# Four edits at the start of a mixture-of-experts stage: tile memory, an earlier second gather group, the scale folded into the stored tokens, block sums dealt out

## The chip, the core and the metric

The kernel runs on 1 core of one Trainium2 chip, as one program. A run's time is the device time of that core, in microseconds (us). Times are told as the median of several runs; the profile is of one further execution.

## The reference, cut to what matters

Two layers work on 512 tokens of width 1024. Each mixes the tokens (layer 0: attention beside pooling; layer 1: spatial gating beside a short convolution), projects the result out, adds it to the stream, and then runs a mixture of 16 experts, of which every token uses two of one group.

```python
h_lat = h_lat + g1 * y                                # y: the mixer with its out-projection
h_lat = h_lat + g2 * hier_moe(modulate(h_lat, norm2_g[i], sh2, sc2), *moe_args)

def modulate(x, gain, shift, scale):
    return rms_norm(x, gain) * (1 + scale) + shift

def hier_moe(t, ...):
    g_idx = top_k(softmax(t @ rg_w + rg_b), 1)        # the group
    top_i = top_k(softmax(e_logits of that group), 2) # two experts in it
    # per expert: y = (silu(t @ wg) * (t @ wu)) @ wd, added with the token's weight
```

## The kernel before, in words

The engines are called by their short names: PE multiplies matrices, DVE and ACT work on vectors, POOL issues gathers and scatters, SP issues the loads of weights. Each engine does its instructions in the order in which they are written.

**Out-projection (out_proj, L1081).** For each of four tiles of 128 tokens (t = 0 to 3) and each half of the width, PE makes 128x512 products; DVE multiplies them by the gate row (L1124, tile yo) and adds them to the stream h (L1125); ACT squares h for the norm (L1127, junk); PE turns h round and forms the router's logits. When a tile has its norm, store (L1151) scales h by it on ACT into a tile u, of which there are three, and sends u to device memory (td, 512 KB a tile), from POOL's queue for t = 0 to 2 and from ACT's for t = 3.

**Routing (route, L1228).** From the logits lg DVE ranks groups and experts (bt, rk, ohg), marks the two chosen (Ab, L1254), PE sums these marks into places (hp), and DVE makes pa (each token's place with each expert) and cnt (tokens of each expert). That is the first part of route; its second part (L1268 to L1300) works out the weights of the tokens and writes them into rec. All tiles of routing lie in the pool "mt", whose memory was in part that of u and of the rest of the out-projection.

**Experts (experts, L1372).** Each expert is a unit with up to 128 tokens, in two halves of 64 (k = 0, 1); the second half runs only if the expert has over 64 tokens. onehot (L1344) makes 128x512 masks oh on DVE; slots (L1352) multiplies them with rec on PE, which gives the tokens' numbers, and DVE decodes them (idxf, idxs, idx); rows (L1582) lets POOL gather 64 double rows of td into a tile gath. unit_t (L1589) then has PE transpose a gathered tile (tp), and ACT and DVE each apply scale and shift to half of it (tf, lines L1601 and L1603: four operations of 128x64 on each, because each column block has a scale and a shift of its own in m2). gu_half (L1610) multiplies tf with the gate and up weights (gu), gated makes hm from it, hidden turns it round (hp, then hf), and down (L1635) multiplies by the down weights (yp), from where DVE weighs the result (ys) and POOL adds it to the stream in device memory.

**The order around the change.** PE, ACT and DVE run in written order in this stage. first_group (L1404) decodes units 0 and 1 one tile at a time, reads the counts into registers (counts, L1465), runs the second part of route, loads ACT's table of silu, and transposes units 0 and 1. Then come unit 0's gate and up products, then second_group (L1427), which makes masks for units 2 and 3 and gathers their tokens, and then the loop over units p. PLAN (L165) is a table of the extra work that follows the gate and up products of unit p + 1: ("o", a) makes masks for units a and a + 1, ("t", a) decodes them, ("w", a) decodes weights, ("r", i) is a third of route_extra (L1302), which counts the further blocks of 128 tokens that crowded experts need. In layer 0 two further blocks are straight units (STRAIGHT = (2, 0)), and the "r" entries are worked off at p = 3, 4 and 5. Layer 1 has none, and there all of route_extra runs at once after p = 5 (end of the loop). Loads of weights go round 16 buffers (raw_any, L258): raw tiles, one raw tile of a pool that reuses u's memory (raw3), halves of h, and the tiles wh and wl.

## Time and profile before

| what | us |
|---|---|
| median of 3 runs (lowest, highest) | 927.77 (925.64, 930.54) |
| the profiled execution | 927.96 |
| its span | 925.8 |
| PE busy in the span | 827.0 (89%) |
| DVE, ACT, POOL busy | 499.4, 335.9, 224.5 |
| mean granted clock of PE | 0.946 of full speed |

The span runs from the first to the last instruction that the profile holds; the 2.2 us around it belong to the execution's time. In the rows below each time is in us from the span's start. In a timeline's row the brackets tell how long the engine was idle just before, and which engine or transfer ended that. SPq, POOLq and ACTq are transfers issued from these engines' queues.

### The profile page before, as it was taken

To read this page: it belongs to the slowest core of one execution; us is meant where nothing else is said; L and a number is where in the kernel's file an instruction comes from. 1 tells how busy PE (TensorE), PEld (TensorE's weight loads), DVE (VectorE), ACT (ScalarE), POOL (GpSimd) and SP (SyncE) were. 2 spreads that over 40 slices of the span, in tenths; PEclk is the share of its full clock that TensorE was granted. 3 is DMA by queue.
4 is the path that set the end of the run, shared out by engine and by line. 5 is a ranking of instruction groups with operands and counts; after the bars stand their busy time and mean duration, and the time that the engine had idled before them with its cause. 6 is when DMAs were issued, how large, how long until landed. Compare 5 with 4: busy or idle time off the path is not lost. (4 is left out here: it accounts for less than half of the span.)

```text
span 925.8 us, 14465 instructions
## 1 busy us (share of the span) xinstructions
PE 827.0 (89%) x5352; PEld 538.3 (58%) x5352; DVE 499.4 (54%) x1236; ACT 335.9 (36%) x710; POOL 224.5 (24%) x196
## 2 busy tenths in 40 slices
PE   6999889999997679999977699999997679899993
PEld 2786557766885345455543487777786335445451
DVE  5467757677344645663322787776444554543330
ACT  4356456557235522223221442223235522222320
POOL 1002220021000234776234000000000255734332
PEclk9999999999999689999999799999999679999997
DMA  9755345454918667999998556882827568999731
GB/s 376 287 195 224 148 166 183 149 182 163 370 59 286 199 210 234 332 319 309 329 318 295 187 205 196 282 306 103 310 111 276 196 233 280 350 318 342 266 44 26
DMA packets 50706, 216.70 MB, mean 234 GB/s; under 512 B 12996, under 2 KB 13508, under 8 KB 32816
## 3 DMA queue, kind: packets, MB, share of 16 engines
q1 hardware_dynamic: 31392, 187.09, 55.0%
q0 software_dynamic: 16736, 21.36, 10.3%
q10 hardware_dynamic: 2480, 6.95, 2.0%
q8 instruction: 60, 0.98, 0.4%
q14 instruction: 38, 0.31, 0.1%
HBM read 207.95 MB, written 26.25 MB: 253 GB/s over the span
## 5 line engine op out<-in xcount | busy, mean ns | idle before, releaser
L1614 PE MATMUL gu<-raw,tf 128*64 128x256 f32 x1072 | 139.4, 400 | 7.5 <-DMA raw<-wgu 4.7
L1614 PEld LDWEIGHTS gu<-raw,tf 128*64 128x64 f32 x1072 | 76.5, 143 | 59.7 <-issue 22.5
L1601 ACT ACTIVATE tf<-tp,m 128x64 f32<-128x64 f32 x192 | 67.0, 401 | 85.2 <-DVE tf L1603 43.7
L1603 DVE TENSOR_SCALAR tf<-tp,m 128x64 f32<-128x64 f32 x192 | 57.1, 339 | 73.6 <-ACT tf L1601 72.6
L290 ACT CAST wh<-raw 128x1024 fp32r<-128x1024 f32 x46 | 48.1, 1049 | 94.8 <-PE acc L609 52.3
L291 DVE TENSOR_TENSOR wl<-raw,wh 128x1024 fp32r<-128x1024 f32 x46 | 55.8, 1219 | 40.1 <-ACT wh L290 40.1
L1641 PE MATMUL yp<-raw,hf 128*64 128x512 f32 x272 | 72.1, 653 | 1.0 <-ACTq L1561 0.4
L1622 ACT ACTIVATE sg<-gu 128x128 f32<-128x128 f32 x48 | 13.3, 277 | 155.2 <-PE gu L1614 120.5
L608 PE MATMUL acc<-xh,wh 128*128 128x512 f32 x160 | 64.2, 402 | 0.3 <-DVE vn L1022 0.3
L610 PE MATMUL acc<-xh,wl 128*128 128x512 f32 x160 | 63.8, 399 | 0.5 <-DVE wl L291 0.5
L609 PE MATMUL acc<-xl,wh 128*128 128x512 f32 x160 | 63.9, 399 | 0.0
L1584 POOL DMA_INDIRECT gath<-td,idx x48 | 52.3, 1089 | 19.5 <-issue 11.0
L1644 DVE SCALAR_TENSOR_TENSOR ys<-yp,w,bc_g 128x512 f32<-128x512 f32 x34 | 25.4, 747 | 52.7 <-PE yp L1641 38.1
L1651 POOL DMA_INDIRECT out<-ys,idx x24 | 37.5, 1564 | 63.1 <-DVE hm L1624 53.1
L1348 DVE TENSOR_TENSOR oh<-cst,pa 128x512 bf16<-128x512 f32 x80 | 50.1, 683 | 0.0
L1651 POOL DMA_INDIRECT hd<-ys,idx x24 | 39.0, 1623 | 34.8 <-DVE hm L1624 14.9
L515 DVE SCALAR_TENSOR_TENSOR acc<-raw,silu_c,acc 128x1024 f32<-128x1024 f32 x28 | 35.8, 1280 | 17.9 <-ACT acc L513 9.2
L1595 PE MATMUL tp<-cst,gath 128*128 128x128 f32 x192 | 34.7, 310 | 11.6 <-DMA gath<-td,idxs 7.5
L537 POOL DMA_DIRECT2D rowd<-row x4 | 2.4, 596 | 173.6 <-DVE row L531 90.5
L1595 PEld LDWEIGHTS tp<-cst,gath 128*128 128x128 f32 x192 | 22.6, 153 | 33.4 <-issue 22.9
L1624 DVE TENSOR_TENSOR hm<-gu,sg 128x128 f32<-128x128 f32 x48 | 13.8, 288 | 47.9 <-ACT sg L1622 47.5
L300 DVE TENSOR_TENSOR pl<-tp,ph 128x384 fp32r<-128x384 f32 x64 | 34.0, 551 | 8.3 <-ACT ph L299 8.0
(318 smaller groups left out, 1748.4 us busy)
## 6 DMA issues: line engine op xcount, KB each, us to landing
raw<-modw SPq DMA_DIRECT2D x48, 1024.0 KB, 6.2
raw<-wgu SPq DMA_DIRECT2D x48, 1024.0 KB, 7.5
raw<-wdn SPq DMA_DIRECT2D x24, 1024.0 KB, 7.1
raw<-wodd SPq DMA_DIRECT2D x10, 1024.0 KB, 6.7
h<-wgu SPq DMA_DIRECT2D x8, 1024.0 KB, 6.6
wh<-wgu SPq DMA_DIRECT2D x12, 512.0 KB, 8.6
wl<-wgu SPq DMA_DIRECT2D x12, 512.0 KB, 7.5
raw<-woe SPq DMA_DIRECT2D x4, 1024.0 KB, 4.8
```

Of the source, the lines that this page charges most:

```text
L291: last_lo = nc.vector.tensor_tensor(lo, src, hi.bitcast(F32), op=ALU.subtract).ins
L608: t.matmul(out, ah, bh, start=start, stop=False, skip_group_check=True)
L609: t.matmul(out, ah, bl, start=False, stop=False, skip_group_check=True)
L610: t.matmul(out, al, bh, start=False, stop=stop, skip_group_check=True)
L1348: self.nc.vector.tensor_tensor(oh, io[:, None, None, :].to_broadcast([128, NT, 2, 64]), pos[:, :, None, None].to_broadcast([128, NT, 2, 64 ...
L1584: self.gather[u] = self.nc.gpsimd.indirect_dma_start(out=self.gbuf[u % len(self.gbuf)][:, k], out_offset=None, in_=self.td, in_offset=bass ...
L1595: nc.tensor.transpose(tp[:, c], g[:, k, c * 128:(c + 1) * 128], self.ident)
L1601: nc.scalar.activation(tf[:, c, cs], tp[:, c, cs], AF.Identity, bias=m[:, 1, j, c:c + 1], scale=m[:, 0, j, c:c + 1])
L1603: nc.vector.tensor_scalar(tf[:, c, cs], tp[:, c, cs], m[:, 0, j, c:c + 1], m[:, 1, j, c:c + 1], op0=ALU.mult, op1=ALU.add)
L1614: self.nc.tensor.matmul(gu[64 * j:64 * j + 64], tf[:, k4, 64 * c:64 * c + 64], ws[c][k4 // 2][:, k4 % 2 * 512 + j * 256:k4 % 2 * 512 + j * ...
L1641: nc.tensor.matmul(yp[64 * c:64 * c + 64], hf[:, 64 * j:64 * j + 64], ws[2][j][:, c * 512:c * 512 + 512], start=(j == 0), stop=(j == 1), t ...
L1651: s = self.nc.gpsimd.indirect_dma_start(out=self.acc, out_offset=bass.IndirectOffsetOnAxis(ap=idx, axis=0), in_=self.ys[p % len(self.ys)][ ...
```

## The change

1. **Tiles.** Routing's first tiles (rec, rk, ohg, Ab, pa, cnt) go into R0, the pool that was current before the experts' pool was opened; E1, E2 and the rest stay in the experts' pool.
2. **Second group.** second_group is called in first_group right behind counts, ahead of unit_t for units 0 and 1 and of the second part of route and the table load. unit_t of unit 2 and the last zeros move to PLAN[0] between "w" and the second "o". zeros reads a constant instead of h.
3. **Scale.** The row of the scale is broadcast to all partitions (bc_s2, a further transfer on POOL), update multiplies h by it into u (scaled, a 128x512 operation on DVE), u has four buffers, store scales u in place. unit_t is then one DVE operation of 128x512 that adds the shift.
4. **Block sums.** Layer 1 works off route_extra by the "r" entries at p = 3, 4 and 5, as layer 0 does.

```diff
-PLAN = {0: (("o", 0), ("w", 0), ("o", 4)), 1: ...
+PLAN = {0: (("o", 0), ("w", 0), ("u", 2), ("o", 4)), 1: ...
...
     def bcasts(self, eng=None):
-        self.bcast("g1", self.bcp, eng)
+        for nm in ("g1", "s2"):
+            self.bcast(nm, self.bcp, eng)
...
+            def scaled(t, half):
+                cs = slice(half * 512, (half + 1) * 512)
+                if not half:
+                    us[t] = S.tile([128, D], F32, name="u", bufs=4)
+                return nc.vector.tensor_tensor(us[t][:, cs], self.h[:, t, cs], self.bc["s2"][:, cs], op=ALU.mult).ins
...
-                last = nc.vector.tensor_tensor(self.h[:, t, cs], self.h[:, t, cs], z, op=ALU.add).ins
+                nc.vector.tensor_tensor(self.h[:, t, cs], self.h[:, t, cs], z, op=ALU.add)
+                last = scaled(t, half)
...
             def store(t, r, q=None):
-                u = S.tile([128, D], F32, name="u", bufs=3)
-                nc.scalar.activation(u, self.h[:, t], AF.Copy, scale=r)
-                (q or nc.gpsimd).dma_start(tdv[t], u)
+                nc.scalar.activation(us[t], us[t], AF.Copy, scale=r)
+                (q or nc.gpsimd).dma_start(tdv[t], us[t])
...
     def moe(self, l):
+            self.R0 = self.R
             R = self.R = self.pool(es, f"mt{l}")
...
     def route(self, R, pp):
+        M, R = R, self.R0
         rec = R.tile([128, NE, NT, 5], BF16, name="rec")
...
-        Ab, E1, E2 = T4("Ab", BF16), T4("E1"), T4("E2")
+        Ab = T4("Ab", BF16)
...
         yield pa, rec, cnt
+        R = M
+        E1, E2 = T4("E1"), T4("E2")
...
             self.regs = counts()
+            second_group()
             zeros(self.gbuf[4:6])
+            for u in range(2):
+                th[u, 0] = self.unit_t(u, 0, S, pp)
             next(rt)
             self.table(AF.Silu)
-            for u in range(2):
-                th[u, 0] = self.unit_t(u, 0, S, pp)
-            zeros(self.gbuf[6:] + [y[:, 1:2] for y in self.ys])
...
-            second_group()
             regs = self.regs
...
+                    if what == "u":
+                        th[2, 0] = self.unit_t(2, 0, S, pp)
+                        zeros(self.gbuf[6:] + [y[:, 1:2] for y in self.ys])
...
                     elif what == "r":
-                        if nst:
-                            rx = rx or self.route_extra(R, tb)
-                            next(rx)
+                        rx = rx or self.route_extra(R, tb)
+                        next(rx)
...
-                if not p:
-                    th[2, 0] = self.unit_t(2, 0, S, pp)
...
-                if p == 5 and not nst:
-                    rx = list(self.route_extra(R, tb))
...
     def unit_t(self, u, k, S, pp):
-        m = self.m2[self.l]
-        for j in range(2):
-            cs = slice(64 * j, 64 * j + 64)
-            for c in range(2):
-                nc.scalar.activation(tf[:, c, cs], tp[:, c, cs], AF.Identity, bias=m[:, 1, j, c:c + 1], scale=m[:, 0, j, c:c + 1])
-            for c in range(2, 4):
-                nc.vector.tensor_scalar(tf[:, c, cs], tp[:, c, cs], m[:, 0, j, c:c + 1], m[:, 1, j, c:c + 1],
-                                        op0=ALU.mult, op1=ALU.add)
+        sh = self.m2[self.l][:, :, :, None].to_broadcast([128, 4, 2, 64])
+        nc.vector.tensor_tensor(tf.rearrange("p c (j s) -> p c j s", j=2), tp.rearrange("p c (j s) -> p c j s", j=2), sh,
+                                op=ALU.add)
```

In the lists of instructions that follow, "..." leaves rows out. First DVE where layer 0's experts begin, before (cnti are the counts, TENSOR_LOAD their reading into registers, E to rec the second part of routing):

```order
L1468 CAST cnti<-cnt 1x16
L1471 TENSOR_LOAD cnti x4
L1270 SCALAR_TENSOR_TENSOR E_3144<-rk,ohg 128x64
L1271 SCALAR_TENSOR_TENSOR E_3145<-rk,ohg 128x64
...
L1299 CAST rec<-wq 128x64
L1603 TENSOR_SCALAR tf<-tp,m_0_103 128x64 x8
L1348 TENSOR_TENSOR oh<-cst,pa 128x512 x4
L1365 TENSOR_REDUCE idxs<-hp 128x4
L1624 TENSOR_TENSOR hm<-gu,sg 128x128
L1348 TENSOR_TENSOR oh<-cst,pa 128x512 x4
```

The same place now, with the lines' new numbers:

```order
L1480 CAST cnti<-cnt 1x16
L1483 TENSOR_LOAD cnti x4
L1360 TENSOR_TENSOR oh<-cst,pa 128x512 x4
L1377 TENSOR_REDUCE idxs<-hp 128x4
L1607 TENSOR_TENSOR tf<-tp,m_0_103 128x512 x2
L1282 SCALAR_TENSOR_TENSOR E_3341<-rk,ohg 128x64
...
L1311 CAST rec<-wq 128x64
L1628 TENSOR_TENSOR hm<-gu,sg 128x128
L1360 TENSOR_TENSOR oh<-cst,pa 128x512 x4
L1381 TENSOR_REDUCE wf_3454<-hp 128x4
L1607 TENSOR_TENSOR tf<-tp,m_0_103 128x512
L1360 TENSOR_TENSOR oh<-cst,pa 128x512 x4
```

The masks and the decoding of the second group (oh, idxs) stand right behind the counts, and the two shift additions (tf) ahead of the second part of routing. hm of unit 0 stands behind that part, as unit 0's gate and up products no longer have the second group behind them; unit 2's tf stands ahead of the masks of the second "o". Layer 1 begins with the same rows.

Second, DVE in layer 1 around the block sums (nb to cx), before:

```order
L1644 SCALAR_TENSOR_TENSOR ys_8241<-yp,w_8745,bc_g_7775 128x512
...
L1307 TENSOR_SCALAR nb<-cnt 128x16
...
L1313 COPY cs<-nb 128x16
L1317 TENSOR_TENSOR cs<-cs 128x16 x4
...
L1330 TENSOR_REDUCE xe<-selt 128x7
L1334 CAST nx<-cs 1x1
...
L1340 TENSOR_REDUCE cx<-selt 1x7
L1624 TENSOR_TENSOR hm<-gu,sg 128x128
L1603 TENSOR_SCALAR tf<-tp,m_1_104 128x64 x4
```

And now:

```order
L1319 TENSOR_SCALAR nb<-cnt 128x16
...
L1325 COPY cs<-nb 128x16
L1360 TENSOR_TENSOR oh<-cst,pa 128x512 x4
...
L1381 TENSOR_REDUCE w_8891<-hp 128x4
L1329 TENSOR_TENSOR cs<-cs 128x16 x4
...
L1342 TENSOR_REDUCE xe<-selt 128x7
L1572 COMPARE_AND_BRANCH
L1607 TENSOR_TENSOR tf<-tp,m_1_104 128x512
...
L1360 TENSOR_TENSOR oh<-cst,pa 128x512 x4
L1346 CAST nx<-cs 1x1
...
L1352 TENSOR_REDUCE cx<-selt 1x7
L1572 COMPARE_AND_BRANCH
```

The 19 operations that stood in one row, between two units, are three pieces behind the decoding or the masks of three units.

Third, SP's loads while layer 0's out-projection ends (h is the stream's tile, used as a buffer for weights; wh and wl too), before:

```order
L255 DMA raw<-wdn 128x2048
L274 DMA wh<-wgu 128x1024
L255 DMA raw<-wgu 128x2048
L274 DMA wh<-wdn 128x1024
L274 DMA wh<-wgu 128x1024
L255 DMA raw<-wgu 128x2048
L269 DMA h<-wgu 128x2048
L274 DMA wl<-wgu 128x1024
...
L269 DMA h<-wdn 128x2048
```

And now:

```order
L255 DMA raw<-wdn 128x2048
L269 DMA h<-wdn 128x2048
L274 DMA wh<-wgu 128x1024
L255 DMA raw<-wgu 128x2048
L274 DMA wh<-wdn 128x1024
L274 DMA wh<-wgu 128x1024
L255 DMA raw<-wgu 128x2048
L269 DMA h<-wgu 128x2048
L274 DMA wl<-wgu 128x1024
```

The 1 MB load `h<-wdn` has moved from behind the wl loads to the front: zeros no longer reads h, so nothing behind the out-projection holds it. Beside these, the fixed order of attention's and pooling's products in layer 0 comes out otherwise on PE, ACT and DVE, with the same products.

## Rows read from the trace of the kernel before

**Rows 1.** The profile page, section 2: the span in 40 equal slices of 23.1 us. Each digit is a tenth: PE's busy share, and the clock that PE was granted.

```profile
PE   6999889999997679999977699999997679899993
...
PEclk9999999999999689999999799999999679999997
```

**Rows 2.** Busy time by stretch. A row gives the stretch and its length, then busy us (and instructions) of PE, of PE's weight loads, of DVE, ACT and POOL, then PE's granted clock, the DMA engines' busy share and GB/s.

```profile
120.00:246.00 126.00, 121.32 (x855) 87.90 (x854) 87.78 (x223) 73.70 (x165) 11.99 (x13) 0.99 0.53 195
...
356.00:470.00 114.00, 111.42 (x867) 58.96 (x863) 57.02 (x169) 31.04 (x101) 66.92 (x50) 1.00 0.99 321
...
766.00:807.30 41.30, 41.23 (x340) 21.77 (x334) 20.34 (x55) 10.81 (x35) 26.79 (x21) 1.00 0.96 325
```

**Rows 3.** Timeline of layer 0 from the last tile's store to the first gate and up products (start, duration, engine, line, operation, count, idle before).

```profile
298.23 0.33 ACTq L1154 DMA_DIRECT2D td<-u  x1
...
301.70 0.33 SPq L255 DMA_DIRECT2D raw<-wgu  x1
303.01 0.23 DVE L1254 SCALAR_TENSOR_TENSOR Ab<-rk,ohg 128x64 bf16<-128x64 f32 x1 [4.09 <-DMA td<-u]
...
305.32 0.15 DVE L1365 TENSOR_REDUCE idxf<-hp 128x1 int32<-128x2 f32 x1
...
306.32 1.58 POOL L1584 DMA_INDIRECT gath<-td,idxf  x1 [2.80 <-DVE idxf L1365]
...
310.41 0.23 DVE L1270 SCALAR_TENSOR_TENSOR E<-rk,ohg 128x64 f32<-128x64 f32 x1 [2.00 <-issue]
...
311.84 1.09 PE L1595 MATMUL tp<-cst,gath 128*128 128x128 f32 x4 [0.26 <-DMA gath<-td,idxf]
...
314.22 5.25 PE L1614 MATMUL gu<-raw,tf 128*64 128x256 f32 x32 [1.29 <-ACT tf L1601]
...
314.85 0.26 DVE L1299 CAST rec<-wq 128x64 bf16<-128x64 f32 x1
```

**Rows 4.** The same timeline, from the second group's masks on.

```profile
318.79 2.49 DVE L1348 TENSOR_TENSOR oh<-cst,pa 128x512 bf16<-128x512 f32 x4
...
321.63 0.17 DVE L1365 TENSOR_REDUCE idxs<-hp 128x4 int32<-128x8 f32 x1 [0.35 <-PE hp L1358]
321.71 0.33 SPq L269 DMA_DIRECT2D h<-wdn  x1
321.89 0.29 DVE L1624 TENSOR_TENSOR hm<-gu,sg 128x128 f32<-128x128 f32 x1
...
322.54 0.33 PE L1630 MATMUL hp<-cst,hm 128*128 128x128 f32 x1
```

**Rows 5.** The timeline of layer 0 from the last weight slots to the transposes of unit 2 and of unit 0's second half.

```profile
324.64 0.25 PE L1358 MATMUL hp<-rec,oh 128*128 128x3 bf16 x4 [0.35 <-DVE oh L1348]
...
328.58 1.97 PE L1595 MATMUL tp<-cst,gath 128*128 128x128 f32 x8 [3.69 <-DMA gath<-td,idxs]
```

**Rows 6.** Timeline of layer 1's first stretch.

```profile
720.75 0.23 DVE L1254 SCALAR_TENSOR_TENSOR Ab<-rk,ohg 128x64 bf16<-128x64 f32 x1 [4.42 <-DMA td<-u]
...
724.01 1.60 POOL L1584 DMA_INDIRECT gath<-td,idxf  x1 [3.11 <-DVE oh L1348]
...
727.88 0.23 DVE L1270 SCALAR_TENSOR_TENSOR E<-rk,ohg 128x64 f32<-128x64 f32 x1 [1.76 <-issue]
...
739.39 0.29 DVE L1624 TENSOR_TENSOR hm<-gu,sg 128x128 f32<-128x128 f32 x1
```

**Rows 7.** Timeline of layer 1, last weight slots and transposes.

```profile
742.15 0.25 PE L1358 MATMUL hp<-rec,oh 128*128 128x3 bf16 x4 [0.35 <-DVE oh L1348]
...
746.18 1.12 PE L1595 MATMUL tp<-cst,gath 128*128 128x128 f32 x4 [3.78 <-DMA gath<-td,idxs]
```

**Rows 8.** Timeline of layer 1 at the block sums, behind unit 5: their first operation, and PE's next two.

```profile
806.46 0.17 DVE L1307 TENSOR_SCALAR nb<-cnt 128x16 f32<-128x16 f32 x1
...
811.66 0.33 PE L1630 MATMUL hp<-cst,hm 128*128 128x128 f32 x1 [4.32 <-DVE hm L1624]
...
811.92 1.57 PE L1614 MATMUL gu<-raw,tf 128*64 128x256 f32 x8
```

**Rows 9.** PE's timeline in layer 0 at the units where the block sums are dealt out there.

```profile
375.15 1.08 PE L1614 MATMUL gu<-wh,tf 128*64 128x256 f32 x8 [0.67 <-DVE ys L1644]
...
388.67 1.08 PE L1614 MATMUL gu<-wl,tf 128*64 128x256 f32 x8 [0.78 <-DVE tf L1603]
```

**Rows 10.** The profile page, section 5: the two groups of operations in unit_t (busy us, mean ns of one, idle time before them and what ended most of it).

```profile
L1601 ACT ACTIVATE tf<-tp,m 128x64 f32<-128x64 f32 x192 | 67.0, 401 | 85.2 <-DVE tf L1603 43.7
L1603 DVE TENSOR_SCALAR tf<-tp,m 128x64 f32<-128x64 f32 x192 | 57.1, 339 | 73.6 <-ACT tf L1601 72.6
```

**Rows 11.** DVE's groups by line and form in 258 to 296 us, layer 0's out-projection.

```profile
L1124 DVE TENSOR_TENSOR yo<-sp,bc_g 128x512 f32<-128x512 f32 x8 | 5.2, 686 | 12.3 <-PE sp L610 12.2
```

**Rows 12.** DVE's waits in the same stretch (us in total, times, longest).

```profile
DVE ss L1137 <- ACT junk L1127: 0.9, 1, 0.9
```

**Rows 13.** Transfers issued in 296 to 332 us: what, from which queue, how many, median us from issue to landing.

```profile
gath<-td,idxf POOLq DMA_INDIRECT x4, 3.7
```

**Rows 14.** PE's waits in 356 to 497 us, the loaded part of layer 0's experts (us in total, times, longest).

```profile
PE gu L1614 <- DMA raw<-wgu: 4.7, 1, 4.7
```

**Rows 15.** PE's waits in 120 to 246 us, layer 0's attention and pooling.

```profile
PE sp L878 <- ACT pe L887: 1.2, 1, 1.2
```

**Rows 16.** ACT's groups by line and form in 140 to 246 us: the exponentials of attention.

```profile
L887 ACT ACTIVATE pe<-sp,nb 128x768 f32<-128x768 f32 x27 | 24.5, 907 | 5.5 <-DVE nb L883 3.9 <-DVE ed L966 1.1 <-DVE ri L915 0.2
```

More of the change, by code (lines that the diff above doesn't have):

```diff
@@ L164 @@
 WE, WR, WS = (32, 20), (0, 0, 4), (12, 24)
-PLAN = {0: (("o", 0), ("w", 0), ("o", 4)), 1: (("t", 4), ("o", 2), ("w", 2), ("o", 6)), 2: (("t", 6), ("o", 8)),
+PLAN = {0: (("o", 0), ("w", 0), ("u", 2), ("o", 4)), 1: (("t", 4), ("o", 2), ("w", 2), ("o", 6)), 2: (("t", 6), ("o", 8)),
         3: (("t", 8), ("r", 0), ("o", 10)), 4: (("t", 10), ("r", 1)), 5: (("o", 12), ("r", 2)), 6: (("t", 12), ("x", 0)),
@@ L369, in setup @@
         self.gather = {}
-        self.m2 = [k.tile([128, 2, 2, 4], F32, name=f"m2_{l}") for l in range(2)]
+        self.m2 = [k.tile([128, 4, 2], F32, name=f"m2_{l}") for l in range(2)]
         self.ends = None
@@ L469, in router_parts @@
         if j0 == 0:
-            nc.vector.tensor_copy(self.m2[l][:, 0], cp)
             nc.vector.tensor_tensor(rw, rw, cp[:, :, :, None].to_broadcast([128, 2, 4, 20]), op=ALU.mult)
             return
-        col = self.m2[l][:, 1]
+        col = self.m2[l].rearrange("p f j -> p j f")
         nc.vector.tensor_copy(col, cp)
@@ L540, in bcasts @@
     def bcasts(self, eng=None):
-        self.bcast("g1", self.bcp, eng)
+        for nm in ("g1", "s2"):
+            self.bcast(nm, self.bcp, eng)
     def bcast(self, nm, pool, eng=None):
         t = pool.tile([128, D], F32, name="bc_" + nm)
-        src = self.rowd[self.l, 0:1, 0:2].rearrange("a j n -> a (j n)")
+        G, j = {"g1": (0, 0), "s2": (1, 0)}[nm]
+        src = self.rowd[self.l, G:G + 1, j:j + 2].rearrange("a j n -> a (j n)")
         (eng or self.nc.gpsimd).dma_start(t, src.to_broadcast([128, D]))
@@ L1101, in out_proj @@
             pl = pp.tile([128, 512], F32, name="po")[:, :80].rearrange("p (t n) -> p t n", n=20)
+            us = {}
             ssq = self.sm.tile([128, 2, NT], F32, name="ssq", bufs=1)
@@ L1443, in zeros @@
                 t = t.rearrange("p b d -> p (b d)")
-                nc.scalar.activation(t, self.h[:, 0, :t.shape[-1]], AF.Copy, scale=0.0)
+                nc.scalar.activation(t, self.ident[:, 0:1].to_broadcast([128, t.shape[-1]]), AF.Copy, scale=0.0)
         def weights(a):
@@ L1516, in experts @@
                 for what, a in PLAN.get(p, ()):
-                    if what == "w":
+                    if what == "u":
+                        th[2, 0] = self.unit_t(2, 0, S, pp)
+                        zeros(self.gbuf[6:] + [y[:, 1:2] for y in self.ys])
+                    elif what == "w":
                         weights(a)
```

## The prediction

> **What bounds the kernel now.** I began with the page's slices. PE is busy at 9 tenths in most of them, with a low in slices 13 and 14 (278 to 324 us) and in 32 and 33 (717 to 764 us), and there its granted clock falls as well [rows 1]. These are the two places where the experts of a layer begin. Next, the stretches: in the middle of the experts PE works in 111.42 of 114.00 us and in 41.23 of 41.30 us, in attention in 121.32 of 126.00 us [rows 2]. An operation taken from DVE or ACT in those stretches is worth nothing; the two starts are where time can be had. So I read their timelines. The reader is to see three stops in each. DVE has ohg done and sits 4.09 us before Ab, until a store of u has landed [rows 3]; in layer 1 it is 4.42 us [rows 6]. Then the second group's masks come on DVE only when units 0 and 1 are under way [rows 4]. And PE stands 3.69 and 3.78 us before the transposes of unit 2, until its gather has landed [rows 5, 7]. A fourth stop is in layer 1 alone: PE waits 4.32 us for hm, while DVE works off the block sums [rows 8].
>
> **Layer 0's start.** I shift the rows along DVE, because all that PE does here hangs on it.
>
> 1. Ab no longer waits: 303.01 - 4.09 = 298.92 us. From Ab to the first idxf are 2.31 us [rows 3], so the first list is there at 301.2. The gather can't follow at once, since it reads td: the last store is issued at 298.23, and Ab's own wait ended with its landing at 303.0. So the 4.09 us of the wait become 303.0 against 306.32, a gain of 3.3 us for the gather, and 4.09 us for what hangs on DVE alone.
> 2. After the counts DVE is free at 310.41 - 4.09 = 306.3 [rows 3]. The masks of the second group now stand there: from their start to idxs 2.84 us [rows 4], so slots and idxs are done by 309.2. They are on the path now, but were on it before as well.
> 3. The gathers of units 0 and 1 start at 303.0 and 1.9 us later (1.58 and a gap of 0.3 on POOL) and land 3.7 us on [rows 3, 13]: 306.7 and 308.6. PE comes to the transposes at 309.1, so they are hidden, with 0.5 to 2 us to spare. Two transposes at 1.09 [rows 3] end at 311.3.
> 4. The additions: 128x512 from PSUM. The nearest row is yo, of that shape and source, at 0.686 us [rows 11]; the eight operations that it replaces took 401 and 339 ns each in turn between ACT and DVE [rows 10]. First products at about 311.1 against 314.22, second addition done at 312.1.
> 5. The second part of routing, from E to the end of rec, took 310.41 to 315.11 = 4.70 us [rows 3]. It now lies behind the additions: 312.1 to 316.8. hm of unit 0 stands behind it, and so starts at 316.8, not at 321.89 [rows 4]: 5.1 us earlier. PE idles some 2 us before it; that is in the sum.
> 6. From hm to the transposes of unit 2 the work is the same up to the last slots (324.64 [rows 5]); the wait of 3.69 us behind them goes, since idxs now is there at 309.2 and its gathers land by 315. Gain at unit 2: 5.1 + 3.69 = **8.8 us**.
>
> **Layer 1's start.** By the same steps: E would be at 727.88 - 4.42 = 723.46 [rows 6]; the masks there instead, idxs 2.84 later at 726.3; first gather at 720.75, when the store has landed, against 724.01; the second's landing at 720.75 + 1.9 + 3.7 = 726.4, no later than PE's turn. Two transposes at the full clock, some 0.65 each, and the addition: 728.3. Routing's second part 4.7: hm at 733.0 against 739.39 [rows 6], 6.4 us; with the wait of 3.78 [rows 7] **10.2 us**.
>
> **Block sums.** The 4.32 us stop goes. Behind it PE took 1.57 us for eight products [rows 8] that take 1.08 us elsewhere [rows 9], since its clock had fallen; with the transposes and down products behind, I estimate the aftermath at 1.3 (0.49 here, and about 0.4 for each of two further groups of such a size). Dealt out, the sums cost what layer 0's show: stops of 0.67 and 0.78 us [rows 9]. 5.6 - 1.45 = **4.2 us**. Bounds: 2.5, if the clock gives nothing back (4.32 - 1.45 = 2.9) and a third piece shows, and 5.6.
>
> **What it costs.** scaled adds a 128x512 operation of about 0.69 us per half tile (by yo [rows 11], as the nearest). Behind it stands the sum of squares ss, which waited for ACT's squaring by 0.9 us [rows 12]; one scaled fits in, for t = 0 and 1 two stand there, so 0.4 us a layer, **0.8 us** in all; bounds 0 and 16 x 0.69 = 11 us, the former nearer, as most of these lie under PE's products (DVE sat 12.2 us before yo [rows 11]). The broadcast of bc_s2 on POOL is wanted only behind attention's 126 us [rows 2] and is priced at nothing; without that cover it would be one more wait of a transfer, some 4 us by [rows 13]. `h<-wdn` moves from 321.71 [rows 4] to the out-projection on SP; it takes its 1 MB out of the start of the experts and puts it beside the out-projection, priced at nothing, with 1 us either way. In the loaded middle the lighter unit_t is priced at nothing, with at most the 2.6 us that PE idles in 114 [rows 2] as a bound. Layer 0's attention comes in another order: its products are the same, and I put 0, bounds -3 and +3 from PE's 4.7 us of idle time there [rows 2].
>
> **The sum.** -8.8 - 10.2 - 4.2 + 0.8 = -22.4 us. The profiled execution took 927.96 us, 0.2 over the median, so 905.6 there and **905.4** for a median.
>
> **Rivals.**
>
> A. Layer 0 gives it back to the stream of weights. For: in 356 to 470 us the DMA engines are busy 0.99 of the time [rows 2], and PE has a stop of 4.7 us for a load behind it [rows 14]; if the stream doesn't start earlier too, that stop grows by all of layer 0's gain. Against: the loads are released when PE gives buffers back, and so shift with it. 905.4 + 8.8 = 914.2. Chance 0.13.
>
> B. The first gathers collide with a load. The load of raw3 was issued at 301.70, when two stores of u had landed, 4.6 us ahead of the first gather [rows 3]; now it and the gather wait for the same last store, and 1 MB goes out beside them. Gathers that take as long again, 3.7 us [rows 13], eat the spare time of 0.5 to 2 us and put off the transposes by some 2.5 us a layer: 910.4. The Trainium skill, "DMA: Bandwidth & Descriptors", section "Queues, rings and completion order", says that each DMA engine takes turns between the queues that have work for it, packet by packet; by that rule the gathers would get about half of the engines for as long as the load is under way, which is the doubling of this case and would make the sum -17.4 in place of -22.4. The rows here don't decide it, as no load went out with the first gathers before. Chance 0.12.
>
> C. The change doesn't free the tiles: R0's memory is held by something else of the out-projection, or the masks oh wait for u's memory in their turn. Then the starts win only the second group's part (the 3.69 and 3.78 us, and its slots) and lose 4.09 and 4.42: 905.4 + 8.5 = 913.9. Chance 0.04.
>
> D. Slower: the new order of layer 0's attention. PE does its rows in order; there it stood 1.2 us for an exponential on ACT, once [rows 15], of 27 at 0.907 us each [rows 16]. If the new order puts products ahead of an exponential that isn't done, each costs about that 1.2 us; all 27 would make 32 us, 937.8. It decides from 23 of the 27 on (22.4 us of gain and 4.6 of margin). Against: PE has work from three other chains there, and idles 4.7 of 126 us. Chance 0.04. With half of them and A, the time would lie at 920 to 928, about no change: 0.05.
>
> **How the numbers follow.** My forecast, 0.62. Down, the aftermath of the block sums and the clock (1.4), the attention (3), and the lighter units (2 to 3) reach to 897; up, A, B and C reach to 915, and A with B to 918. Range 897 to 918. The measurement can tell about 0.5%, 4.6 us: faster below 923.1, slower above 932.4. Forecast, A, B and C lie below 923: 0.91; D above: 0.04; the mixture between: 0.05.
>
> **What would show it.** In the changed profile: Ab right behind ohg in both layers, with no wait on td<-u; first gathers when the last store has landed, some 3.3 us earlier; idxs ahead of the first gu; no wait of PE before unit 2's transposes; a stop of some 2 us of PE before unit 0's hm, behind routing's second part; in layer 1 no stop of over 1 us at the block sums; ACT's share of unit_t gone, with PE's busy time in the middle unchanged. The forecast is wrong if Ab or oh waits as long as before, if the gathers take over 6 us, if the stop for a load in layer 0 [rows 14] grows by the start's gain, or if PE's idle time in layer 0's attention grows by over 5 us.

## The result, and the profile after

| what | us |
|---|---|
| changed kernel, median of 4 runs (lowest, highest) | 895.78 (891.66, 899.29) |
| kernel before, beside it, 4 runs | 926.70 (922.86, 930.54) |
| ratio, 95% interval | 0.967 (0.961 to 0.972) |
| the profiled execution of the changed kernel, its span | 899.29, 897.4 |
| PE busy; DVE, ACT, POOL busy | 822.4 (92%); 486.1, 272.4, 224.3 |
| mean granted clock of PE | 0.957 |

The change makes the kernel 30.9 us faster. The forecast was 22.4 us; the time lies 1.2 us below the low end of the range. The direction and the places were right; the size was not. In the tables below, one run far above the others of its kernel (927.87 us in u_group, 956.65 in x_warm, 934.99 in a_tiles) is counted in the median, but not in the ratio.

The page's slices of the changed kernel, against [rows 1]; a slice is now 22.4 us:

```profile
PE   6999989999999689999979499999999689999992
...
PEclk9999999999999799999989799999999689999997
```

Each of the two lows reads 6 and 8 where 7, 6 and 7 stood. The timeline of layer 0's start shows what went, against [rows 3, 4]:

```profile
298.28 0.33 ACTq L1162 DMA_DIRECT2D td<-u  x1
299.02 0.23 DVE L1264 SCALAR_TENSOR_TENSOR Ab<-rk,ohg 128x64 bf16<-128x64 f32 x1
...
302.48 0.33 SPq L255 DMA_DIRECT2D raw<-wgu  x1
...
303.27 1.14 POOL L1593 DMA_INDIRECT gath<-td,idxf  x1 [8.33 <-DVE oh L1360]
...
306.34 2.50 DVE L1360 TENSOR_TENSOR oh<-cst,pa 128x512 bf16<-128x512 f32 x4 [1.97 <-issue]
...
309.03 1.95 PE L1604 MATMUL tp<-cst,gath 128*128 128x128 f32 x8
309.20 0.17 DVE L1377 TENSOR_REDUCE idxs<-hp 128x4 int32<-128x8 f32 x1 [0.36 <-PE hp L1370]
...
310.97 6.49 PE L1618 MATMUL gu<-raw,tf 128*64 128x256 f32 x40
...
311.62 0.21 DVE L1282 SCALAR_TENSOR_TENSOR E<-rk,ohg 128x64 f32<-128x64 f32 x1
...
315.48 0.26 DVE L1311 CAST rec<-wq 128x64 bf16<-128x64 f32 x1
316.65 0.28 ACT L1626 ACTIVATE sg<-gu 128x128 f32<-128x128 f32 x1 [1.98 <-PE gu L1618]
316.96 0.29 DVE L1628 TENSOR_TENSOR hm<-gu,sg 128x128 f32<-128x128 f32 x1 [1.22 <-ACT sg L1626]
...
319.83 1.07 PE L1604 MATMUL tp<-cst,gath 128*128 128x128 f32 x8
...
320.83 1.94 PE L1645 MATMUL yp<-raw,hf 128*64 128x512 f32 x8
```

Ab has no bracket any more: it doesn't wait. PE's transposes at 309.03 and those of unit 2 at 319.83 have none either; the latter stood at 328.58 behind a wait of 3.69 us [rows 5]. Layer 1's start has the same steps, against [rows 6, 7]:

```profile
704.97 0.22 DVE L1264 SCALAR_TENSOR_TENSOR Ab<-rk,ohg 128x64 bf16<-128x64 f32 x1
...
709.47 1.09 POOL L1593 DMA_INDIRECT gath<-td,idxf  x1 [9.32 <-DVE idxf L1377]
...
716.90 6.62 PE L1618 MATMUL gu<-raw,tf 128*64 128x256 f32 x40
...
723.02 0.29 DVE L1628 TENSOR_TENSOR hm<-gu,sg 128x128 f32<-128x128 f32 x1 [1.36 <-ACT sg L1626]
...
725.88 0.64 PE L1604 MATMUL tp<-cst,gath 128*128 128x128 f32 x4
```

At layer 1's block sums, in three pieces from 759 to 776 us, PE has one stop left, against 4.32 us [rows 8]:

```profile
764.40 1.08 PE L1618 MATMUL gu<-wh,tf 128*64 128x256 f32 x8 [0.93 <-DVE hm L1628]
```

And PE's waits over the whole span, by what is waited for (us in total, times, longest):

```profile
PE gu L1618 <- DMA raw<-wgu: 4.6, 1, 4.6
PE tp L902 <- ACT pe L888: 2.4, 1, 2.4
...
PE hp L1634 <- DVE hm L1628: 2.1, 4, 1.1
```

The load stop of layer 0 is as long as before [rows 14]. Attention has one stop for an exponential, of 2.4 us.

I cut both profiled executions at marks that both have (the first yo of a layer's out-projection; the layer's second hp made from hm, which belongs to unit 0's second half in layer 0 and to unit 1 in layer 1; the last hp of a layer) and set the stages beside the forecast:

| stage, us | before | after | difference | forecast |
|---|---|---|---|---|
| start to layer 0's first yo | 259.05 | 259.09 | 0.0 | 0 |
| to the second hp | 79.60 | 69.63 | -10.0 | -8.4 |
| to the last hp of layer 0 | 155.59 | 155.08 | -0.5 | 0 |
| to layer 1's first yo | 181.96 | 180.50 | -1.5 | 0 |
| to the second hp | 78.05 | 67.34 | -10.7 | -9.8 |
| to the last hp of layer 1 | 154.76 | 148.69 | -6.1 | -4.2 |

That is -28.7 against -22.4. The profiled execution of after lay 3.5 us above its median and that of before 0.2 above the one that the forecast was set against; 6.3 + 3.5 - 0.2 = 9.6 us are the whole distance from 905.4 to 895.8.

### The profile page after: what moved, and what is told of

Read it like the earlier page. It is cut to its first block, busy times and chain, and to the rows that moved or that the text cites. A ratio compares the mean times of both kernels' runs of the same rounds, so it can differ in the third digit from the quotient of the medians.

```text
span 897.4 us, 14068 instructions
## 1 busy us (share of the span) xinstructions
PE 822.4 (92%) x5352; PEld 535.7 (60%) x5352; DVE 486.1 (54%) x1106; ACT 272.4 (30%) x518; POOL 224.3 (25%) x198
## 5 line engine op out<-in xcount | busy, mean ns | idle before, releaser
L1645 PE MATMUL yp<-raw,hf 128*64 128x512 f32 x272 | 68.4, 625 | 0.4 <-ACT hf L1636 0.4
L1607 DVE TENSOR_TENSOR tf<-tp,m 128x512 f32<-128x512 f32 x48 | 33.0, 688 | 23.9 <-PE tp L1604 23.7
L609 PEld LDWEIGHTS acc<-xh,wh 128*128 128x128 f32 x160 | 30.3, 189 | 10.4 <-issue 1.7
L882 DVE TENSOR_REDUCE mx<-sp 128x1 f32<-128x768 f32 x32 | 30.4, 951 | 10.4 <-PE sp L879 10.4
L299 ACT CAST ph<-tp 128x384 fp32r<-128x384 f32 x64 | 29.8, 484 | 19.6 <-PE tp L902 19.3
```

The lines of the kernel that those rows point to most:

```text
L609: t.matmul(out, ah, bh, start=start, stop=False, skip_group_check=True)
L1645: nc.tensor.matmul(yp[64 * c:64 * c + 64], hf[:, 64 * j:64 * j + 64], ws[2][j][:, c * 512:c * 512 + 512], start=(j == 0), stop=(j == 1), t ...
```

## Experiments

The kernels stand in four sets, each run beside the kernel before: the four named u_; x_unit8, x_mid8, x_warm and a_tiles; x_after, x_mid8dve, a_scale and t_bcast; x_after2, x_mid8b, x_lateb and x_mask. The kernel before took 924.4 us in the first set and 935.7 to 937.2 in the others, so ratios are compared across sets, and times only within one. zeros reads a constant in all of them but t_bcast.

**One edit undone at a time** (first set).

```diff
 u_tiles
-        M, R = R, self.R0
+        M = R
 u_group
             self.regs = counts()
-            second_group()
 ...
             th.pop((0, 0))
+            second_group()
 u_scale (and bcasts, update, store as before)
-        nc.vector.tensor_tensor(tf..., tp..., sh, op=ALU.add)
+        for j in range(2): ... (four operations on ACT, four on DVE, scale and shift)
 u_sums
+                        if nst:
                             rx = rx or self.route_extra(R, tb)
                             next(rx)
 ...
+                if p == 5 and not nst:
+                    rx = list(self.route_extra(R, tb))
```

u_tiles: 

> The changed kernel with part 1 undone: all of routing's tiles back in the experts' pool. The forecast's first step (the pool frees Ab) says that Ab waits for a store again, 4.1 and 4.4 us, and that the time rises by about 8 us. Its rival: part 3 alone has moved the memory (four tiles u in place of three), Ab waits for none in either case, and the time is that of the changed kernel within 1.5 us. The trace tells: Ab's idle time in both layers.

u_group: 

> The changed kernel with part 2 undone: second group behind unit 0's products, routing's second part and the table load ahead of units 0 and 1's transposes. The forecast's account has here the two waits of 3.7 us before unit 2's transposes and some 1 us of masks and slots in each layer: 9 to 10 us slower than the changed kernel. A second account adds PE's clock: the wait halves it for the down products behind, 1.7 us more in each layer: 12 to 14 us slower.

u_scale: 

> The changed kernel with part 3 undone: shift and scale in eight operations again, no scaled, three tiles u. The forecast prices scaled at 0.8 us and the lighter unit_t in the loaded middle at nothing, so this would be 0.8 us faster than the changed kernel. The trace of the changed kernel shows no time for scaled and steps of 0.1 to 0.3 us gained at most units; by that account it is 3 to 5 us slower.

u_sums: 

> The changed kernel with part 4 undone: layer 1's block sums in one row behind unit 5. The forecast: 4.2 us slower (4.32 of stop and 1.3 of slower clock, less 1.45 for the dealt pieces). By the trace of the changed kernel the dealt pieces cost one stop of 0.9 us: 4.8 to 5.0 us slower.

| kernel | us | ratio to before (95%) | against u_tiles |
|---|---|---|---|
| u_tiles | 894.96 | 0.967 (0.964 to 0.970) | 0 |
| u_group | 903.92 | 0.977 (0.974 to 0.981) | +9.0 |
| u_scale | 910.16 | 0.985 (0.981 to 0.988) | +15.2 |
| u_sums | 899.68 | 0.974 (0.972 to 0.977) | +4.7 |

u_tiles is as fast as the changed kernel: edit 1 does nothing that edit 3 hadn't done. In DVE's timeline of u_tiles Ab has no wait in either layer, although it is in the old pool:

```profile
301.25 0.22 DVE L1264 SCALAR_TENSOR_TENSOR Ab<-rk,ohg 128x64 bf16<-128x64 f32 x1
...
705.36 0.23 DVE L1264 SCALAR_TENSOR_TENSOR Ab<-rk,ohg 128x64 bf16<-128x64 f32 x1
```

Edit 3 brings a fourth buffer of u and the tile bc_s2, which would put the tiles behind them at other addresses (t_bcast, below, shows what such a tile does; no run read the addresses). u_group cost the 9 us that the forecast's account gives. The waits are back, but at half their size; PE's timeline in u_group, both layers:

```profile
322.16 1.97 PE L1604 MATMUL tp<-cst,gath 128*128 128x128 f32 x8 [1.94 <-DMA gath<-td,idxs]
...
728.07 1.12 PE L1604 MATMUL tp<-cst,gath 128*128 128x128 f32 x4 [1.79 <-DMA gath<-td,idxs]
```

The missing half goes with the load `h<-wdn`. The first gather of these units on POOL, in the kernel before and then in u_group:

```profile
322.54 1.11 POOL L1584 DMA_INDIRECT gath<-td,idxs  x1 [10.68 <-ACT sg L1622]
```

```profile
318.06 1.51 POOL L1593 DMA_INDIRECT gath<-td,idxs  x1 [9.81 <-DVE hm L1628]
```

In the kernel before, the 1 MB load goes out 0.8 us ahead of that gather in both layers (at 321.71 [rows 4] and 739.22 us), and PE's transposes come 6.0 and 6.1 us behind the gather. In u_group zeros reads the constant, the load has moved, and it is 4.1 and 4.0 us. The two kernels made from the one before agree: 3.7 and 3.9 us in a_scale, which has the constant, 6.7 and 6.4 in t_bcast, which hasn't. So some 2 us of each of the waits of [rows 5, 7] belong to a load beside the gathers. No kernel has the constant undone alone.

u_sums brings back the stop of [rows 8], and 4.7 us:

```profile
784.30 0.33 PE L1637 MATMUL hp<-cst,hm 128*128 128x128 f32 x1 [4.33 <-DVE hm L1631]
```

u_scale is 15.2 us slower, where 0.8 faster was expected by the forecast's two terms and 3 to 5 slower by the trace. Both left out the starts, although the forecast's steps 4 and 5 have the short addition there. By the marks of the table above, against u_tiles, 5.9 and 4.5 us of the 15.0 between the two profiles lie in the starts (74.94 against 69.08, 70.09 against 65.60), 1.9 in layer 1's later units (149.70 against 147.84) and none in layer 0's (154.25 against 154.21); the other 2.8 lie outside the experts. The three undone costs add up to 28.9 of the 29.4 us, although the freed Ab is in none of them; so they overlap.

**One edit alone, on the kernel before.** a_tiles has edit 1, a_scale edit 3; t_bcast only adds the tile bc_s2 and its transfer, which nothing reads.

```diff
 a_tiles
+        M, R = R, self.R0
         (and zeros on the constant)
 a_scale
+        edit 3 as in the change
 t_bcast
-        self.bcast("g1", self.bcp, eng)
+        for nm in ("g1", "s2"):
+            self.bcast(nm, self.bcp, eng)
```

a_tiles: 

> The kernel before with part 1 alone (and zeros reading the constant). Ab no longer waits 4.1 and 4.4 us. The first gather is then held by the store's landing, 3.3 us earlier than before in each layer, and what follows comes as much earlier: 6 to 7 us faster than before, if nothing else steps in; the second group's waits stay.

a_scale: 

> The kernel before with part 3 alone (and zeros reading the constant). If the fourth tile u frees Ab as the pool of part 1 does, Ab doesn't wait in either layer and this kernel has all of the forecast's step 1 besides the lighter units: 6 to 7 us for Ab, 3.6 for the units, some 4 for the short chain at the starts, together 14 to 16 us faster than before. If Ab needs part 1, 6 to 9.

t_bcast: 

> The kernel before with the broadcast of the scale's row alone, which nothing reads. It brings another order of attention in layer 0, as the change does (the stop for a load in it goes, one for an exponential of 2.4 us comes). If the order is worth what one profile shows, 0 to 1.5 us faster; the forecast has 0, the remainder of part 3 (16.6 less 9.5 us) would ask for up to 7.

a_tiles: 925.08 us (916.6 to 935.0), ratio 0.984 (0.979 to 0.989), some 15 us faster by the ratio, twice what was expected, with wide scatter. a_scale: 920.0 us, 0.982 (0.978 to 0.986), 17 us faster, a little over what was expected. Ab doesn't wait in a_scale either (301.75 and 713.97 us), so edits 1 and 3 each free it, and their gains hold the same waits. t_bcast: 931.59 us, 0.995 (0.992 to 0.998), 4.9 us faster. It was to price a transfer, and is confounded: the tile of 4 KB a partition moved the later ones, and Ab stands without a wait there too, as DVE's timeline shows:

```profile
299.38 0.23 DVE L1256 SCALAR_TENSOR_TENSOR Ab<-rk,ohg 128x64 bf16<-128x64 f32 x1
...
720.98 0.22 DVE L1256 SCALAR_TENSOR_TENSOR Ab<-rk,ohg 128x64 bf16<-128x64 f32 x1
```

What the transfer itself costs is not told. Nor is why a_tiles gains three times as much as t_bcast, though both free Ab: the constant in zeros, which only a_tiles has, takes some 2 us off each layer's wait for the second group, and the rest is open.

**What of edit 3 pays?** x_unit8 keeps scale in the stored tokens, but adds the shift by eight operations of 128x64, as before; x_mid8 does so for units behind the third alone; x_mid8dve does those eight on DVE; x_mid8b is x_mid8 again, beside x_after2, the changed kernel again (x_after is its first repeat).

```diff
 x_unit8
-        nc.vector.tensor_tensor(tf..., tp..., sh, op=ALU.add)
+        for j in range(2):
+            for c in range(2):
+                nc.scalar.activation(tf[:, c, cs], tp[:, c, cs], AF.Identity, bias=m[:, c, j:j + 1])
+            for c in range(2, 4):
+                nc.vector.tensor_scalar(tf[:, c, cs], tp[:, c, cs], m[:, c, j:j + 1], None, op0=ALU.add)
 x_mid8, x_mid8b
+        if u > 2:
+            (the eight)
 x_mid8dve
+        if u > 2:
+            for c in range(4):
+                nc.vector.tensor_scalar(...)
```

x_unit8: 

> The changed kernel, with the shift added by the eight old operations (four on ACT, four on DVE, with the scale still folded into the stored tokens). Undoing all of part 3 cost about 15 us. If they lie in the chain of the eight operations, at the starts (about 9 us: the chain of 3.3 us stands ahead of routing's second part and ahead of unit 0's second half) and at the units (about 4 us), this kernel is 11 to 15 us slower than the changed one. If they lie in what else part 3 brings (a new order of attention, bc_s2, four tiles u), it is within 3 us of it.

x_mid8: 

> The changed kernel, with the eight old operations from unit 3 on and the one operation for units 0 to 2. The forecast prices the lighter unit_t in the loaded middle at nothing: equal to the changed kernel within 1 us. The trace of the kernel before shows hf behind operations of tf on ACT; if PE waits for that, 0.1 to 0.3 us at most units: 3 to 4 us slower.

x_mid8dve: 

> The changed kernel, with the shift added by eight operations from unit 3 on, all eight on DVE, none on ACT. If PE's small stops at the units come from hf, which stands behind the operations of tf on ACT, they are gone and the time is the changed kernel's within 1 us, although DVE has more work than in any other kernel here. If they come from the length of the chain of eight, it is 3 to 4 us slower, as the form with four on each engine was.

x_after: 

> The changed kernel once more, as the reference for the runs beside it: 0.966 to 0.969 of the kernel before.

x_mid8b: 

> The eight operations from unit 3 on, beside the changed kernel on one chip: 3 to 4 us slower by the account of small stops at the units, 0 by the forecast.

x_after2: 

> The changed kernel as the reference beside the other three: 0.966 to 0.969 of the kernel before.

| kernel | us | ratio to before (95%) |
|---|---|---|
| x_unit8 | 915.10 | 0.977 (0.972 to 0.982) |
| x_mid8 | 909.97 | 0.971 (0.966 to 0.975) |
| x_mid8dve | 908.86 | 0.971 (0.966 to 0.976) |
| x_after | 905.95 | 0.968 (0.964 to 0.971) |
| x_mid8b | 908.38 (907.7 to 909.6) | 0.971 (0.968 to 0.974) |
| x_after2 | 905.87 (905.3 to 906.6) | 0.967 (0.964 to 0.970) |

Eight additions in place of one cost 0.977 less 0.968, some 9 us. They are not quite the old eight operations: without the scale they take 313 ns on ACT and 277 on DVE (median of one), with it 403 and 339 in u_scale. x_unit8 and x_mid8 differ in units 0 to 2 alone, and x_unit8 is 5.1 us slower, 2.1 and 1.7 of it in the two starts by the marks. In x_unit8's timeline of layer 0's start, the eight operations of units 0 and 1 keep DVE and ACT in turns ahead of E, which comes at 313.26 us, and PE stops before the products of unit 0's second half:

```profile
310.53 6.44 PE L1622 MATMUL gu<-raw,tf 128*64 128x256 f32 x40
...
313.26 0.21 DVE L1282 SCALAR_TENSOR_TENSOR E<-rk,ohg 128x64 f32<-128x64 f32 x1
...
325.97 4.54 PE L1622 MATMUL gu<-raw,tf 128*64 128x256 f32 x40 [3.01 <-ACT tf L1610]
```

But x_mid8b, where the starts are as in the changed kernel, is 2.5 us slower than x_after2, and their runs don't overlap; x_mid8dve is 2.9 us slower than x_after, with runs that do. In the two profiles the difference shows in layer 1's last stage, 156.0 against 153.1 us. Of these 2.9 us, 1.3 lie in one stretch behind unit 1's hp, in which x_after, without the eight, is as long as x_mid8b (14.80, 14.79, and 13.51 in x_after2). PE has no long wait for tf there: the longest is 0.8 us, where x_after2 stands 0.4. The reader has to look at one unit in detail. A loaded unit in the kernel before:

```profile
450.42 0.33 PE L1630 MATMUL hp<-cst,hm 128*128 128x128 f32 x1
...
450.88 0.70 ACT L1601 ACTIVATE tf<-tp,m 128x64 f32<-128x64 f32 x2 [0.67 <-DVE tf L1603]
451.47 0.26 ACT L1632 COPY hf<-hp 128x128 f32<-128x128 f32 x1
...
451.83 0.65 PE L1641 MATMUL yp<-raw,hf 128*64 128x512 f32 x2
```

The same unit in the changed kernel:

```profile
439.60 0.33 PE L1634 MATMUL hp<-cst,hm 128*128 128x128 f32 x1
...
439.97 0.27 ACT L1636 COPY hf<-hp 128x128 f32<-128x128 f32 x1 [1.57 <-PE hp L1634]
...
440.77 1.89 PE L1645 MATMUL yp<-raw,hf 128*64 128x512 f32 x8
```

And in x_mid8b:

```profile
448.03 0.33 PE L1643 MATMUL hp<-cst,hm 128*128 128x128 f32 x1
448.19 0.52 ACT L1611 ACTIVATE tf<-tp,m 128x64 f32<-128x64 f32 x2 [0.54 <-DVE tf L1613]
...
448.59 0.27 ACT L1645 COPY hf<-hp 128x128 f32<-128x128 f32 x1
...
449.20 1.89 PE L1654 MATMUL yp<-raw,hf 128*64 128x512 f32 x8
```

Before, hf stood behind two of tf's operations on ACT and came 1.05 us after hp began; now it comes 0.37 after, and yp 1.17 after hp in place of 1.41. That is 0.24 us in such a unit. Elsewhere the stop is 0.1 to 0.45 us, or nothing, and over layer 1's later units it comes to 1.1 us. u_scale, with the old operations, has it again (1.42). x_mid8b has not: its shorter operations let hf come 0.56 after hp, and yp comes 1.17 after it, as in the changed kernel; in x_mid8dve, with none on ACT, it is 1.18. So the 2.5 us of x_mid8b are not this stop, and what makes them stays open.

**The clock at the starts.** x_warm puts more throw-away products on PE behind the steps of routing, so that it doesn't idle there.

```diff
-                    self.warm(2, m)
+                    self.warm(2 if n < 4 else 6, m)
 ...
+                m = self.slots(...)
+                if (u, k) != pairs[-1]:
+                    self.warm(2, m)
```

x_warm: 

> The changed kernel with more idle products on PE (four more behind the last list of the first group, two behind each of three lists of the second), so that its clock is up when unit 0's products begin. If the half clock holds unit 0's products (6.5 us for 40 in place of 4.5) and these hold hm, hm comes 1 to 1.2 us earlier in each layer, until routing's second part holds it: 2 to 2.5 us faster. If routing's second part holds hm, as step 5 of the forecast has it, no change.

908.69 us, 0.969 (0.964 to 0.974): no gain over x_after's 0.968. The clock did rise, to 1.00 over unit 0's products where the changed kernel has 0.69, as its timeline shows:

```profile
311.07 4.54 PE L1620 MATMUL gu<-raw,tf 128*64 128x256 f32 x40 [0.23 <-issue]
...
316.14 0.28 ACT L1628 ACTIVATE sg<-gu 128x128 f32<-128x128 f32 x1 [1.59 <-PE gu L1620]
316.45 0.29 DVE L1630 TENSOR_TENSOR hm<-gu,sg 128x128 f32<-128x128 f32 x1 [0.71 <-ACT sg L1628]
316.79 0.33 PE L1636 MATMUL hp<-cst,hm 128*128 128x128 f32 x1 [1.18 <-DVE hm L1630]
```

The 40 products took 4.54 in place of 6.49 us, but hp came 17.92 us after Ab, against 18.37 in the changed kernel's first profile, and 17.6 to 19.6 in the other kernels here with the same work ahead of it. No gain is clear of that scatter, and neither account had the size. PE now stands 1.18 us in front of hp.

**Two variants on the changed kernel.** x_lateb sends bc_s2 later, from ACT's queue; x_mask moves the masks of units 4 and 5 behind unit 0's second half.

```diff
 x_lateb
-        for nm in ("g1", "s2"):
-            self.bcast(nm, self.bcp, eng)
+        self.bcast("g1", self.bcp, eng)
 ...
             us = {}
+            s2 = ... nc.scalar.dma_start(s2, ...)
 x_mask
-PLAN = {0: (("o", 0), ("w", 0), ("u", 2), ("o", 4)), 1: (("t", 4), ...
+PLAN = {0: (("o", 0), ("w", 0), ("u", 2)), 1: (("o", 4), ("t", 4), ...
```

x_lateb: 

> The changed kernel, with the row of the scale broadcast later, at the out-projection's start from ACT's queue: attention in layer 0 then has the order of the kernel before on PE, DVE and ACT, and everything behind it is the changed kernel's. If the new order is worth what the profiles of both orders show (a stop for a load of 2.7 to 4.0 us and some lost clock against a stop of 2.4 us), 0.5 to 3 us slower than the changed kernel; the forecast has 0. If the new order brings all that is unexplained, 4 to 8 us slower.

x_mask: 

> The changed kernel with the masks of the second o entry moved from behind unit 0 to the front of unit 1's work. In the changed kernel they stand on DVE ahead of the addition for unit 0's second half, for which PE waits 1.5 us in layer 0: 1 to 1.5 us faster than the changed kernel if nothing is late behind it, no change if the stop moves to unit 1.

x_lateb: 909.33 us, 0.971 (0.968 to 0.974), 3.5 slower than x_after2. Its profile doesn't lay that at layer 0's broadcast: the first yo is 1.5 us earlier than in x_after2, and the excess lies in layer 0's later units, where the code is the same, and between the layers, where layer 1's broadcast is gone too (2.0 and 3.3 us). This stays open. x_mask: 907.27 us, 0.969 (0.965 to 0.973), no gain, though it does what it was made for. The products of unit 0's second half in x_mask, and then in x_after2:

```profile
322.45 4.49 PE L1618 MATMUL gu<-raw,tf 128*64 128x256 f32 x40
```

```profile
324.82 3.46 PE L1618 MATMUL gu<-raw,tf 128*64 128x256 f32 x30 [1.48 <-DVE tf L1607]
```

The stop is gone and PE is 2.4 us ahead, 1.3 of it from ahead of the first yo. By 416 us it is 0.6 behind: in 345 to 425 us x_mask has the DMA engines busy 1.00 of the time, and waits for a load that x_after2 doesn't wait for (PE's waits in that stretch):

```profile
PE gu L1618 <- DMA raw<-wdn: 2.3, 1, 2.3
```

In these two profiles that is rival A in small: time won at layer 0's start is given back to the stream of weights.

## Why the prediction came out as it did

**Layer 0's start, right step by step.** Ab came at 299.02 (forecast 298.92), the first gather at 303.27 (303.0), the second group's masks at 306.34 (306.3), idxs at 309.20 (309.2), PE's transposes at 309.03 without a wait (309.1), the first products at 310.97 (311.1), unit 2 gained 8.75 (8.8).

**Step 5 had the right time by luck.** hm came at 316.96 (316.8), but not behind routing's second part, which took 4.1 us, not 4.7, and ended at 315.74. The 40 products of PE held it, which took 6.49 us at a mean granted clock of 0.69, and PE had no stop before hp, where the forecast put some 2 us. x_warm shows how near the two holders lie: with these products at full clock hm came no earlier than the kernels scatter by.

**The clock was left out.** From the transposes of unit 2 to the hp of unit 0's second half layer 0 took 8.89 us against 10.07, though a new stop of 1.49 us stands there before that half's products. Unit 0's down products took 1.94 us, at a granted clock of 1.00 (2.4 GHz). Before, behind the wait of [rows 5], they had run at 0.50 (1.2 GHz):

```profile
330.48 3.68 PE L1641 MATMUL yp<-raw,hf 128*64 128x512 f32 x8
```

Those 1.2 us and scaled, priced at 0.4 a layer, are what layer 0's start gained beyond the forecast. scaled cost nothing: the first yo is at the same time, and the last store of u is issued at 298.28 against 298.23. Layer 1 shows both signs of the clock. The transposes ahead of hm were put at full clock and ran at 0.50, the products at 0.67 (6.62 us for 40), so that hm came 4.5 us earlier in its stage, not 6.0; behind it came 6.2, where only the wait of 3.78 was put. The starts' 1.6 and 0.9 us beyond the forecast are no more than what kernels with the same start scatter by (69.1 to 70.8 us in layer 0, 65.6 to 67.3 in layer 1).

**Step 6 had the right gain with one cause missing.** The waits of 3.69 and 3.78 us were put down to the late masks. u_group shows that some 2 us of each came from `h<-wdn` beside the gathers, whose move was priced at nothing. The sum is right, since idxs came ahead of both.

**The failing step: "In the loaded middle the lighter unit_t is priced at nothing".** PE's 111.42 of 114 us [rows 2] were read as a cover. Stops of 0.1 to 0.45 us before yp hide in such a share, and the lighter unit_t takes them away. Beside the block sums, layer 1's later units gained 1.2 us (6.07 less 4.83), nearly all of it these stops. u_scale, with the old operations back, lost 1.9 us there; x_mid8b lost 2.5 in all, but not by these stops. In layer 0's later units nothing of the kind shows (155.59 before, 155.08 after; 156.26 us in x_mid8b, 156.79 in x_after2). The bound of 2.6 us, from the idle time that the row shows, was of the right size: a price of 1 to 2 us belonged in the sum, not in the range alone.

**How far that reaches.** Of the 9.6 us between the forecast and the median, 1.2 are the lighter units, 2.5 the starts (the clock, and scaled) and 0.6 the block sums. Another 2.0 lie in stages that the forecast put at nothing, and 3.3 are the distance of the two profiled executions from their medians. So the failing step is one of several small terms, and none of them alone carries the time out of the range.

**Block sums:** 4.8 us in the trace (4.4 and 1.4 won at two units, 0.9 lost at another) and 4.7 by u_sums, forecast 4.2.

**Edit 1 does what the forecast says, but isn't needed.** The forecast took Ab's wait for a matter of the pool. u_tiles and t_bcast show that a tile elsewhere, even one that nothing reads, frees Ab as well. That speaks for addresses, which no run read. The time is the same; the cause given was too narrow.

**The rivals.** A: no, the load stop is 4.6 us as before; but x_mask gave its gain back there. In u_group, too, layer 0's later units are 5.0 us shorter than in u_tiles behind a start that is 4.7 longer; u_sums, though, with layer 0 as in the changed kernel, has them 2.6 shorter, so that these profiles alone don't settle it. B: no. The load was issued 0.79 us ahead of the first gather; the first gathers landed in 4.2 us, not 3.7, and the transposes did not wait. The forecast says that the rows don't decide this rival; but [rows 4] has a load just ahead of the second gathers, and by u_group that costs some 2 us, against the 3.7 of the rival. By the turn by turn rule of the Trainium skill ("DMA: Bandwidth & Descriptors", "Queues, rings and completion order") the forecast had estimated a doubling; the measurement is an eighth more. C: no. D: one stop of 2.4 us for an exponential, with the wait of 2.7 us for a load of modulation weights gone from the same stage; its sum is 0.0.

**Not settled.** u_scale costs 15.2 us and x_unit8 some 9. u_scale's operations are longer, its starts are 5.9 and 4.5 us longer than u_tiles', and the products of unit 0's second half, behind a longer stop, ran at a granted clock of 0.72, where x_unit8's ran at 1.00:

```profile
331.36 6.22 PE L1615 MATMUL gu<-raw,tf 128*64 128x256 f32 x40 [3.59 <-ACT tf L1602]
```

How much each of these makes no run tells. The 1.5 us between the layers are within what that stage scatters by (179 to 186 us over the kernels here that have the same code there), and the 3.5 us by which the profiled execution lies over the median are no term of anything.

## What to carry to other kernels

A busy share near 1 says that no long stop is there, not that the vector engines are free: follow one unit of a loop from one product to the next, and add up its small stops over the units. A kernel made to price them must have the stops in its own trace: x_mid8b, made from shorter operations, had none. Where a stop goes at a start, look at the clock of the products behind it, and at whether the next load was ready for them. Before a wait on a tile's memory is put down to its pool, see whether an unrelated tile frees it too: then the edit that was made for it is worth nothing. And look at what loads go out beside a gather before its whole wait is put down to the gather's late start.

## What the runs showed of the hardware

- The kernel before took 924.4 and 926.7 us in two sets of runs and 935.7 to 937.2 in three others, while the changed kernel's ratio stayed at 0.967 to 0.968. Part of the difference lies in layer 0's experts: in 345 to 425 us x_after2 has PE busy 74.18 us at a granted clock of 0.96, the first profile of the same kernel 78.47 at 1.00. The cause is not shown; the DMA engines are busy 0.97 and 0.98 of that stretch.
- A tile of 4 KB a partition, which nothing reads, made the kernel before 4.9 us faster, with the waits of 4.09 and 4.42 us before Ab [rows 3, 6] gone.
- Products at a granted clock of 1.00 in place of 0.69 (4.54 against 6.49 us for 40) gave the chain that hung on them nothing clear of its scatter, and nothing to the time.
- A 1 MB load issued 0.3 to 0.8 us ahead of four small gathers goes with 2 to 3 us more from the first gather to the products that need it: 6.0 to 6.7 us in the kernel before and t_bcast, 3.7 to 4.1 in u_group and a_scale, in both layers.
